# A list scheduler charges VectorE more, and the sums of a weight matrix are formed early in the kernel

## The chip, the cores and the metric

The kernel runs on one core of a Trainium2 chip. The metric is the device time of one execution in microseconds (us), the median of several runs. A core has five engines with a queue each: PE (TensorE, matrix products), DVE (VectorE), ACT (ScalarE), POOL (GpSimd) and SP (SyncE, which here only issues DMAs). Each engine works through its own list of instructions in order; semaphores make one wait for another.

## The reference, cut to what matters

One decoder layer over 1024 tokens of width 1024, in float32. Two causal token mixers read one projection of the normalised input: mixer A attends to the 256 best keys of each query, which an indexer chooses; mixer B is attention with a forgetting term. Both are gated, merged, and put through `w_out`.

```python
h = rmsnorm(x, g_pre[i])
proj = h @ w_in[i]
(qa, ka, va, gate_a, qi, ki, wi, qb, kb, vb, fb, gate_b) = jnp.split(proj, offs, axis=-1)
...
att_a = dsa_branch(qa, ka, va, qi, ki, wi).reshape(B, S, WIDTH_A)   # indexer scores, top-k, softmax attention
y_a = (att_a * jax.nn.silu(gate_a)) @ w_branch_a[i]
...
att_b = fox_branch(qb, kb, vb, log_f).reshape(B, S, WIDTH_B)
y_b = (att_b * jax.nn.silu(gate_b)) @ w_branch_b[i]
m_a, m_b = jnp.split(jax.nn.sigmoid(h @ w_merge[i]), 2, axis=-1)
out = (m_a * y_a + m_b * y_b) @ w_out[i]
x = x + rmsnorm(out, g_post[i])
e = p[i] @ w_ple[i]
gate = jax.nn.sigmoid(x @ w_ple_gate[i])
x = x + rmsnorm(gate * e, g_ple[i])
```

## The kernel before, in words

Every float32 product is made of three products of rounded parts (high by high, high by low, low by high; the helper `mm3`). So each operand is split first: one engine casts it to the high part, another subtracts that from the source to get the low part (`split_w`, `split_p`). Matrix products are up to 512 columns wide and write 128x512 results into one of eight PSUM banks.

The order of the work is not written by hand. The kernel records its operations (`Program.rec`), and `Program.schedule` then places them one by one on the five engines: a list scheduler, which keeps for each engine the time at which it comes free, and takes the operation that can start first (by priority where several can). How long an operation holds its engine it takes from `_cost`, in ns. For VectorE that is about 69 + 1.04 per column (85 + 1.04 per column for `tensor_tensor_reduce`), with 60 more for a per-partition scalar. To this come fixed latencies from engine to engine (`LAT`). Operations that two engines can do (`any`, `either`, `cast`, `split_w`) go to the one that the scheduler expects to finish first. The scheduler also gives every tile its place in three arenas, so all tiles have the names arena_r (rounded float32 in SBUF), arena_f (float32 in SBUF) and arena_p (PSUM) in the profile, and all instructions that it places have one line, L541.

The stages, in the order of time: the input is normalised, transposed and projected; the indexer's scores are made, with mixer B's value projection (`v_b`, PSUM tiles pv_0 to pv_7) between them; mixer A's query projection (`q_a`, tiles pa_0 to pa_7); then four pairs of heads of mixer B (`pair_b`), during which the top-k search (`top_k`) runs on ACT and DVE in 32 rounds: ACT counts five of the six score blocks against a threshold (`count`), DVE the sixth, and five operations of 6 columns on DVE choose the next threshold. Then come mixer A (`mixer_a`), the branch products, the product with `w_out` and the end. Two projections are filler for PE during the mixers, since nothing waits for them: mixer A's gate (`gates_a`) and the 16 merge gates (`merge_gates`).

The product with `w_out` is made of seven block products (Strassen's scheme in a variant of Winograd) and needs sums of blocks of `w_out`. `weight_sums` forms them: for each of four k, two DMAs bring 2 x 512 KB into a tile of 128x4x512, four subtractions of 128x512 work in it, and a DMA of 1 MB stores it to the DRAM tensor tw_d, which is read back near the end. Before, the subtractions are fixed to POOL (`G.tensor_sub`), and the loads may not start before merge gates 8 to 11 have been recorded as begun (`gate_at[8:12]`), in the late part of mixer A.

Of the kernel before, what the change touches and what calls it, by code (L numbers as in the profile page):

```python
# [150 lines left out]

def _cost(eng, method, a, k):

    if method == "dma_start":
        return 1000.0 if eng == "G" else 475.0
    out = k.get("out", a[0] if a else None)
# [8 lines left out]
    if eng == "A":  # L165
        c = n * 0.833 + 55
# [436 lines left out]
def hybrid_block_kernel(ctx: ExitStack, tc: tile.TileContext, x, p, w_in, b_forget, w_branch_a,  # L603
# [6 lines left out]
    pg = Program(tc, QUOTA)  # L610
    V, A, G, T, SY = pg.V, pg.A, pg.G, pg.T, pg.S
# [400 lines left out]
    def either(method, *a):  # L1012
        pg.any(("G", method, a, {}), ("V", method, a, {}))
# [157 lines left out]
    def q_a():  # L1171
        wqa = load_wn(C_QA, "wqa")
        for b in range(NB):
            psq = pg.psum([P, 512], "d", f"pa_{b}")
            nat_proj(psq, lambda k: wqa[k], b)
            for g in range(2):
                SY.dma_start(qsa_d[b][g], f(q_stack(psq[:, g * 256:g * 256 + 256], b, f"qa{b}{g}", 0.125)))

    def v_b():
        wvb = load_wn(C_VB, "wvb")  # L1180
        for b in range(NB):
            ps = pg.psum([P, 512], "d", f"pv_{b}")
            nat_proj(ps, lambda k: wvb[k], b)
            vt = pg.tile([P, 8, P], F32R, "vbt", f"vb{b}")
            split_p(ps.rearrange("p (h d) -> p h d", d=HD), vt[:, :, 0:HD], vt[:, :, HD:P])
            SY.dma_start(vb_d[:, b], f(vt))
# [73 lines left out]

    pg.at("vb", None)
    v_b()
    pg.at("qa", None)
    q_a()
    pg.at("ga", None)
    gates_a()
    pg.at("mg", None)
    merge_gates()
    pg.at("tw", None)
    tw_d = [pg.dram(dr, [P, 4, 4, 512], "tw_d0")]  # L1270

    def weight_sums(w, dst, after):
        for k in range(4):
            b4 = pg.tile([P, 4, 512], F32, "tw", f"tw{k}")
            for g in range(2):
                SY.dma_start(b4[:, 2 * g:2 * g + 2].rearrange("p a b -> p (a b)"), w[(4 * g + k) * P:(4 * g + k + 1) * P, :])
                pg.ops[-1].deps.add(after[k])
            G.tensor_sub(b4[:, 0], b4[:, 1], b4[:, 0])
            G.tensor_sub(b4[:, 1], b4[:, 3], b4[:, 1])
            G.tensor_sub(b4[:, 3], b4[:, 3], b4[:, 0])  # L1280
            G.tensor_sub(b4[:, 2], b4[:, 2], b4[:, 3])
            SY.dma_start(dst[:, k], b4)

    weight_sums(w_out[0], tw_d[0], gate_at[8:12])
    for pr in range(4):
        pg.at("pair", 1 + pr)
        pair_b(pr)
# [303 lines left out]
```

## Time and profile before

| | before |
|---|---|
| median of 3 runs | 1084.13 us (1083.5 to 1084.75) |
| profiled execution | 1086.23 us |
| its span, first to last instruction | 1084.3 us |
| PE busy | 1058.4 us (98%) |
| DVE busy | 822.1 us (76%) |
| ACT busy | 634.2 us (58%) |
| POOL busy | 122.6 us (11%) |
| mean granted clock of PE | 0.991 |

The busy time of an engine is the time in which one of its instructions ran. PE is busy in nearly all slices; its clock is granted at one of two levels, 1.00 (2.4 GHz) or 0.50 (1.2 GHz). The 1.9 us between the span and the profiled execution's time lie outside the instructions.

### The profile page before, as it was taken

How to read it: one execution, taken by the hardware profiler on the slowest of the kernel's cores; microseconds unless marked ns; L12 is line 12 of the kernel's file. 1: busy time of each engine (PE TensorE's matmuls, PEld its weight loads, DVE VectorE, ACT ScalarE, POOL GpSimd, SP SyncE). 2: the span in 40 equal slices, each digit the busy share in tenths (PEclk: the TensorE clock that was granted, in tenths of full speed). 3: DMA queues.
4: the chain of work that ended last, by engine and by line, in shares of the span. 5: the costliest groups of instructions: out<-in, count | busy, mean ns of one | idle time of the engine just before them, and what ended most of it. 6: DMA issues, size and time to landing. Idle time of an engine off the chain costs nothing. (4 is left out here: it accounts for less than half of the span.)

```text
span 1084.3 us, 16365 instructions
## 1 busy us (share of the span) xinstructions
PE 1058.4 (98%) x5266; PEld 873.1 (81%) x5266; DVE 822.1 (76%) x2136; ACT 634.2 (58%) x1454; POOL 122.6 (11%) x231
## 2 busy tenths in 40 slices
PE   8999999999999999999999999999999999999996
PEld 6887888887878778788787888778888888888885
DVE  7998777658868779889999976774358885598367
ACT  7576668888778788786348866544111243356222
POOL 2000000011201111211130110133010000000000
PEclk9999999999999999999999999999999999999998
DMA  7321143440551622815333431365597436536123
GB/s 250 89 60 49 75 159 108 153 101 20 135 119 59 146 69 69 194 40 186 107 108 116 119 88 59 113 227 204 169 308 237 141 119 211 181 110 197 38 97 117
DMA packets 119945, 139.51 MB, mean 129 GB/s; under 512 B 11819, under 2 KB 76715, under 8 KB 119349
## 3 DMA queue, kind: packets, MB, share of 16 engines
q1 hardware_dynamic: 108292, 120.13, 34.6%
q0 software_dynamic: 11568, 18.35, 7.4%
q8 instruction: 41, 0.67, 0.3%
q14 instruction: 44, 0.35, 0.1%
HBM read 96.94 MB, written 37.32 MB: 124 GB/s over the span
## 5 line engine op out<-in xcount | busy, mean ns | idle before, releaser
L541 PE MATMUL arena_p<-arena_r 128*128 128x512 f32 (+4 forms) x4360 | 1001.3, 384 | 14.3 <-DVE arena_r L541 6.8
L541 PEld LDWEIGHTS arena_p<-arena_r 128*128 128x128 f32 x4360 | 774.1, 189 | 170.0 <-ACT arena_f L541 9.8
L541 DVE TENSOR_TENSOR arena_r<-arena_p,arena_r 128x512 fp32r<-128x512 f32 (+2 forms) x232 | 142.4, 623 | 43.8 <-ACT arena_r L541 40.0
L541 ACT CAST arena_r<-arena_p 128x512 fp32r<-128x512 f32 (+3 forms) x217 | 107.5, 513 | 106.3 <-PE arena_p L541 97.8
L541 ACT ACTIVATE arena_f<-arena_p 128x512 f32<-128x512 f32 (+4 forms) x173 | 89.0, 525 | 129.9 <-PE arena_p L541 127.2
L541 ACT ACTIVATE arena_f<-arena_f,cnd 128x1024 bf16<-128x1024 f32 (+4 forms) x160 | 149.6, 935 | 23.6 <-DVE cnd L541 19.3
L541 DVE TENSOR_TENSOR arena_r<-arena_f,arena_r 128x512 fp32r<-128x512 f32 (+5 forms) x240 | 145.8, 622 | 12.8 <-PE arena_p L541 4.9
L541 ACT CAST arena_r<-arena_f 128x512 fp32r<-128x512 f32 (+3 forms) x144 | 80.4, 584 | 90.3 <-DVE arena_f L541 33.0
L541 ACT ACTIVATE arena_f<-arena_f,stats 128x512 f32<-128x512 f32 (+3 forms) x192 | 116.9, 611 | 27.4 <-DVE stats L541 26.6
L541 PE MATMUL arena_p<-ident,arena_f 128*128 128x128 f32 x720 | 108.7, 275 | 1.5 <-DVE arena_r L541 0.8
L541 PEld LDWEIGHTS arena_p<-ident,arena_f 128*128 128x128 f32 x720 | 87.2, 141 | 22.5 <-DVE arena_r L541 1.6
L541 POOL TENSOR_TENSOR arena_r<-arena_f,arena_r 128x512 fp32r<-128x512 f32 (+1 forms) x29 | 40.3, 1393 | 336.6 <-ACT arena_r L541 258.8
L541 DVE CAST arena_r<-arena_f 128x512 fp32r<-128x512 f32 (+4 forms) x125 | 47.7, 390 | 31.6 <-DMA arena_f<-in_w_out_dram 9.7
L541 DVE CUSTOM_DVE_ANT_0 arena_f<-arena_p,arena_f 128x512 f32<-128x512 f32 (+2 forms) x112 | 64.4, 578 | 7.6 <-PE arena_p L541 4.3
L541 DVE TENSOR_TENSOR arena_f<-arena_f 128x512 f32<-128x512 f32 (+3 forms) x132 | 64.9, 496 | 3.1 <-DMA arena_f<-rd_d 2.0
L541 ACT COPY arena_f<-arena_p 64x256 f32<-64x256 f32 (+5 forms) x94 | 42.5, 452 | 32.5 <-PE arena_p L541 27.3
L541 POOL TENSOR_SCALAR_AFFINE_SELECT arena_f<-arena_f 128x128 f32<-128x128 f32 x70 | 21.6, 309 | 314.2 <-DVE stats L541 112.7
L541 DVE CAST arena_r<-arena_p 128x512 fp32r<-128x512 f32 (+4 forms) x67 | 41.9, 626 | 19.8 <-PE arena_p L541 17.2
L541 DVE SCALAR_TENSOR_TENSOR arena_f<-arena_f,wi 128x384 f32<-128x384 f32 (+3 forms) x70 | 45.9, 657 | 12.7 <-ACT arena_f L541 12.1
L541 DVE SCALAR_TENSOR_TENSOR arena_f<-arena_f,arena_p 128x512 f32<-128x512 f32 x48 | 32.9, 685 | 24.9 <-PE arena_p L541 18.7
L541 DVE SCALAR_TENSOR_TENSOR arena_f<-arena_f 128x512 f32<-128x512 f32 (+8 forms) x48 | 29.3, 614 | 27.3 <-ACT arena_f L541 27.2
L541 ACT ACTIVATE arena_f<-arena_f 128x512 bf16<-128x512 f32 (+2 forms) x41 | 28.2, 687 | 27.1 <-DVE arena_f L541 24.5
(101 smaller groups left out, 514.8 us busy)
## 6 DMA issues: line engine op xcount, KB each, us to landing
arena_f<-in_w_in_dram SPq DMA_DIRECT2D x56, 256.0 KB, 3.7
arena_f<-in_w_merge_dram SPq DMA_DIRECT2D x32, 256.0 KB, 3.1
th_d<-arena_f SPq DMA_DIRECT2D x32, 256.0 KB, 2.0
arena_f<-th_d SPq DMA_DIRECT2D x32, 256.0 KB, 3.3
arena_f<-in_w_out_dram SPq DMA_DIRECT2D x14, 512.0 KB, 3.7
arena_f<-in_x_dram SPq DMA_DIRECT2D x18, 256.0 KB, 6.5
vb_d<-arena_r SPq DMA_DIRECT2D x8, 512.0 KB, 2.6
qsa_d<-arena_r SPq DMA_DIRECT2D x16, 256.0 KB, 2.4
```

Of the source, the lines that this page charges most:

```text
L541: getattr(eng[x], m)(*[real(q) for q in a], **{n: real(q) for n, q in k.items()})
```

## The change

`_cost` becomes `_hold`, and a new `_cost` wraps it: for VectorE an operation costs at least 100 ns, and one with an accumulator output (`accum_out`) costs 100 ns more. The other engines' costs stay as they are. The weight sums are recorded right behind `v_b`, their loads may start with the first four blocks of mixer B's value projection (`vb_at[:4]`), and each subtraction may go to POOL or VectorE (`either`). `gate_at` is still filled, and no longer read.

```diff
 def _cost(eng, method, a, k):

+    c = _hold(eng, method, a, k)
+    return max(c, 100.0) + (100.0 if "accum_out" in k else 0.0) if eng == "V" else c
+
+
+def _hold(eng, method, a, k):
     if method == "dma_start":
         return 1000.0 if eng == "G" else 475.0
...
+    vb_at = []
+
     def v_b():
         wvb = load_wn(C_VB, "wvb")
         for b in range(NB):
+            vb_at.append(len(pg.ops))
             ps = pg.psum([P, 512], "d", f"pv_{b}")
...
     pg.at("vb", None)
     v_b()
+    pg.at("tw", None)
+    tw_d = [pg.dram(dr, [P, 4, 4, 512], "tw_d0")]
+
+    def weight_sums(w, dst, after):
+        for k in range(4):
+            b4 = pg.tile([P, 4, 512], F32, "tw", f"tw{k}")
+            for g in range(2):
+                SY.dma_start(b4[:, 2 * g:2 * g + 2].rearrange("p a b -> p (a b)"), w[(4 * g + k) * P:(4 * g + k + 1) * P, :])
+                pg.ops[-1].deps.add(after[k])
+            either("tensor_sub", b4[:, 0], b4[:, 1], b4[:, 0])
+            either("tensor_sub", b4[:, 1], b4[:, 3], b4[:, 1])
+            either("tensor_sub", b4[:, 3], b4[:, 3], b4[:, 0])
+            either("tensor_sub", b4[:, 2], b4[:, 2], b4[:, 3])
+            SY.dma_start(dst[:, k], b4)
+
+    weight_sums(w_out[0], tw_d[0], vb_at[:4])
     pg.at("qa", None)
...
-            G.tensor_sub(b4[:, 0], b4[:, 1], b4[:, 0])
-            G.tensor_sub(b4[:, 1], b4[:, 3], b4[:, 1])
-            G.tensor_sub(b4[:, 3], b4[:, 3], b4[:, 0])
-            G.tensor_sub(b4[:, 2], b4[:, 2], b4[:, 3])
-            SY.dma_start(dst[:, k], b4)
-
-    weight_sums(w_out[0], tw_d[0], gate_at[8:12])
```

Since every later decision of the scheduler follows from the costs, nearly all lists change. The total of PE's instructions does not; 12 of POOL's 46 subtractions, additions and products go to DVE, and 20 casts go from DVE to ACT. Three places follow.

ACT's list, in the second pair of mixer B. `ACTIVATE arena_f,cnt` are counts of the search (128x1024 down to 128x512 are one round), `ACTIVATE arena_r<-arena_p 64x512 x2` empties a query projection out of its PSUM bank, `CAST arena_r<-arena_p` and `COPY` empty other banks. Before:

```order
L541 CAST arena_r<-arena_p 64x512
L541 CAST arena_r<-arena_f 128x512 x2
L541 ACTIVATE arena_f,cnt<-arena_f,cnd 128x1024
L541 ACTIVATE arena_f,cnt<-arena_f,cnd 128x896
L541 ACTIVATE arena_f,cnt<-arena_f,cnd 128x768
L541 ACTIVATE arena_r<-arena_p 64x512 x2
L541 ACTIVATE arena_f,cnt<-arena_f,cnd 128x640
L541 ACTIVATE arena_f,cnt<-arena_f,cnd 128x512
```

The same place now:

```order
L546 ACTIVATE arena_f,cnt<-arena_f,cnd 128x512
L546 ACTIVATE arena_f,cnt<-arena_f,cnd 128x1024
L546 ACTIVATE arena_r<-arena_p 64x512 x2
L546 ACTIVATE arena_f,cnt<-arena_f,cnd 128x896
L546 ACTIVATE arena_f,cnt<-arena_f,cnd 128x768
L546 ACTIVATE arena_f,cnt<-arena_f,cnd 128x640
L546 ACTIVATE arena_f,cnt<-arena_f,cnd 128x512
```

The emptying of the query projection stood behind three counts of its round, and stands behind one.

PE's list, in the third pair's key projection, while the second pair's last head is finished. `MATMUL arena_p<-ident,arena_f` are transposes of probabilities, of which `x4` opens the head's output, `128x512` are projections or the first products of probabilities and values. Before, the first of these products are the 4th and 5th of the row `x8`:

```order
L541 MATMUL arena_p<-ident,arena_f 128x128 x4
L541 MATMUL arena_p<-arena_r 128x128 x2
L541 MATMUL arena_p<-ident,arena_f 128x128 x3
L541 MATMUL arena_p<-arena_r 128x512 x6
L541 MATMUL arena_p<-ident,arena_f 128x128 x2
L541 MATMUL arena_p<-arena_r 128x512 x8
```

Now they are the 4th and 5th of the row `x14`:

```order
L546 MATMUL arena_p<-ident,arena_f 128x128 x4
L546 MATMUL arena_p<-arena_r 128x512 x3
L546 MATMUL arena_p<-arena_r 128x256 x2
L546 MATMUL arena_p<-ident,arena_f 128x128 x3
L546 MATMUL arena_p<-arena_r 128x128 x2
L546 MATMUL arena_p<-arena_r 128x512 x15
L546 MATMUL arena_p<-ident,arena_f 128x128 x2
L546 MATMUL arena_p<-arena_r 128x512 x14
```

Between the transposes and the product that needs them, split, stood 9 matmuls of 128x512 and stand 21.

SP's list, beside mixer B's value projection. `in_w_in_dram 128x512` are loads of the weights of mixer A's query projection, `128x4x128` of other projections, `vb_d` are stores of mixer B's values. Before, no load of `w_out` stands here:

```order
L541 DMA arena_f<-in_w_in_dram 128x4x128 x2
L541 DMA vb_d<-arena_r 128x1024
L541 DMA arena_f<-in_w_in_dram 128x512 x3
L541 DMA vb_d<-arena_r 128x1024
L541 DMA arena_f<-in_w_in_dram 128x512 x2
L541 DMA arena_f<-in_w_in_dram 128x4x128
```

Now the last two of four rounds of the weight sums read:

```order
L546 DMA arena_f<-in_w_out_dram 128x1024 x2
L546 DMA vb_d<-arena_r 128x1024 x2
L546 DMA arena_f<-in_w_in_dram 128x4x128 x2
L546 DMA tw_d_146<-arena_f 128x2048
L546 DMA arena_f<-in_w_out_dram 128x1024 x2
L546 DMA vb_d<-arena_r 128x1024
L546 DMA arena_f<-in_w_in_dram 128x512 x4
L546 DMA vb_d<-arena_r 128x1024 x2
L546 DMA tw_d_146<-arena_f 128x2048
L546 DMA arena_f<-in_w_in_dram 128x512
```

The last load of the query weights, the eighth, now stands behind the last store of the sums, and behind whatever that store waits for. All 16 subtractions of the sums are on DVE here, the last of them during the first matmuls of the query projection; in mixer A, POOL's rows `TENSOR_TENSOR arena_f<-arena_f 128x512 x4` and `x12` are gone.

## Rows read from the trace of the kernel before

**Rows 1.** Page: busy time of engines, and PE's clock in 40 slices.

```profile
PE 1058.4 (98%) x5266; PEld 873.1 (81%) x5266; DVE 822.1 (76%) x2136; ACT 634.2 (58%) x1454; POOL 122.6 (11%) x231
...
PEclk9999999999999999999999999999999999999998
```

**Rows 2.** Busy time by stage (count of instructions), PE's clock, DMA share, GB/s.

```profile
80.00:160.00 80.00, 80.00 (x376) 64.28 (x375) 60.98 (x131) 52.21 (x105) 1.57 (x4) 1.00 0.29 95
160.00:240.00 80.00, 80.00 (x391) 66.33 (x391) 52.77 (x204) 66.32 (x138) 4.83 (x8) 1.00 0.44 129
240.00:510.00 270.00, 261.20 (x1342) 216.26 (x1341) 221.09 (x634) 220.94 (x526) 44.16 (x96) 0.99 0.39 101
510.00:600.00 90.00, 88.06 (x430) 72.01 (x429) 84.06 (x201) 47.12 (x128) 17.79 (x16) 0.98 0.37 114
600.00:740.00 140.00, 137.06 (x699) 111.33 (x698) 105.13 (x275) 83.39 (x214) 28.67 (x30) 0.99 0.40 125
```

**Rows 3.** PE's timeline at five waits: start, length, what; idle before it.

```profile
248.62 0.65 PE L541 MATMUL arena_p<-arena_r 128*128 128x384 f32 x1 [2.39 <-DVE arena_f L541]
...
306.68 0.73 PE L541 MATMUL arena_p<-arena_r 128*128 128x512 f32 x1 [1.92 <-DVE arena_r L541]
...
365.67 0.50 PE L541 MATMUL arena_p<-arena_r 128*128 128x512 f32 x1 [0.97 <-DVE arena_r L541]
...
521.10 1.52 PE L541 MATMUL arena_p<-arena_r 128*128 128x128 f32 x5 [1.50 <-DVE stats L541]
...
725.13 1.19 PE L541 MATMUL arena_p<-arena_r 128*128 128x512 f32 x4 [1.96 <-DVE arena_r L541]
```

**Rows 4.** A stretch of 128x512 matmuls alone, and two stretches of lower clock.

```profile
760.00:800.00 40.00, 40.00 (x178) 33.14 (x177) 12.48 (x27) 5.73 (x11) 4.94 (x9) 1.00 0.71 217
...
306.70:310.10 3.40, 3.40 (x8) 2.72 (x9) 2.73 (x8) 3.31 (x7) 0.00 (x0) 0.50 0.40 96
...
726.60:730.00 3.40, 3.40 (x11) 2.72 (x10) 1.30 (x2) 0.60 (x1) 0.00 (x0) 0.50 0.39 154
```

**Rows 5.** Timeline ahead of the wait at 306.68, ACT and DVE.

```profile
301.83 1.04 ACT L541 ACTIVATE arena_f<-arena_f,cnd 128x896 bf16<-128x896 f32 x1
...
303.00 0.94 ACT L541 ACTIVATE arena_f<-arena_f,cnd 128x768 bf16<-128x768 f32 x1
...
303.93 1.18 ACT L541 ACTIVATE arena_r<-arena_p 64x512 fp32r<-64x512 f32 x2
...
305.15 1.39 DVE L541 SCALAR_TENSOR_TENSOR arena_r<-arena_p,arena_r 64x512 fp32r<-64x512 f32 x2 [3.24 <-ACT arena_r L541]
```

**Rows 6.** Timeline ahead of the wait at 725.13, DVE and POOL.

```profile
718.58 0.69 DVE L541 TENSOR_TENSOR arena_r<-arena_p,arena_r 128x512 fp32r<-128x512 f32 x1
719.18 0.68 DVE L541 TENSOR_TENSOR arena_f<-arena_f 128x512 f32<-128x512 f32 x1
...
720.00 5.61 POOL L541 TENSOR_TENSOR arena_f<-arena_f 128x512 f32<-128x512 f32 x4 [7.84 <-DMA th_d<-arena_f]
...
721.56 1.44 DVE L541 CAST arena_r<-arena_f 128x128 fp32r<-128x128 f32 x2
...
722.92 1.55 DVE L541 TENSOR_TENSOR arena_r<-arena_f,arena_r 128x128 fp32r<-128x128 f32 x2
```

**Rows 7.** Groups by shape: count, busy time, mean ns of one, idle before.

```profile
L541 DVE DVE_READ_ACCUMULATOR2_ANT stats<- 128x1 f32 x193 | 15.9, 82 | 0.0
...
L541 DVE CAST arena_r<-arena_f 128x128 fp32r<-128x128 f32 x25 | 6.3, 263 | 0.3 <-DMA va_d<-arena_r 0.3
```

**Rows 8.** DVE's timeline: a reduction, its accumulator's read, and the next reduction.

```profile
248.48 0.74 DVE L541 CUSTOM_DVE_ANT_0 arena_f<-arena_p,arena_f,stats 128x512 f32<-128x512 f32 x1
249.15 0.08 DVE L541 DVE_READ_ACCUMULATOR2_ANT stats<- 128x1 f32 x1
249.15 0.68 DVE L541 CUSTOM_DVE_ANT_0 arena_f<-arena_p,arena_f 128x512 f32<-128x512 f32 x1
```

**Rows 9.** Page, DMA issues: count, KB each, median us to landing.

```profile
arena_f<-in_w_in_dram SPq DMA_DIRECT2D x56, 256.0 KB, 3.7
```

More of the change, by code (lines that the diff above doesn't have):

```diff
@@ L1262, in hybrid_block_kernel @@
     v_b()
[L1263 to L1268, printed above, removed]
     pg.at("tw", None)
@@ L1277, in weight_sums @@
                 pg.ops[-1].deps.add(after[k])
-            G.tensor_sub(b4[:, 0], b4[:, 1], b4[:, 0])
-            G.tensor_sub(b4[:, 1], b4[:, 3], b4[:, 1])
-            G.tensor_sub(b4[:, 3], b4[:, 3], b4[:, 0])
-            G.tensor_sub(b4[:, 2], b4[:, 2], b4[:, 3])
+            either("tensor_sub", b4[:, 0], b4[:, 1], b4[:, 0])
+            either("tensor_sub", b4[:, 1], b4[:, 3], b4[:, 1])
+            either("tensor_sub", b4[:, 3], b4[:, 3], b4[:, 0])
+            either("tensor_sub", b4[:, 2], b4[:, 2], b4[:, 3])
             SY.dma_start(dst[:, k], b4)
-    weight_sums(w_out[0], tw_d[0], gate_at[8:12])
+    weight_sums(w_out[0], tw_d[0], vb_at[:4])
+    pg.at("qa", None)
+    q_a()
+    pg.at("ga", None)
+    gates_a()
+    pg.at("mg", None)
+    merge_gates()
     for pr in range(4):
```

## The prediction

> **What bounds the kernel now.** I read the page first: PE is busy for 98% of the span, at full clock in nearly every slice [rows 1]. So the change, which leaves PE's instructions as they are, can only win or lose what PE stands still or runs slowly; VectorE's and POOL's busy time count only where PE waits for them. Then I cut the busy time into stages [rows 2]: from 80 to 240 us PE has no idle time that the rows show, from 240 to 740 us, the two mixers, it lacks 8.80 + 1.94 + 2.94 = 13.7 us. The third view is PE's timeline at its long waits [rows 3]: five of them, 2.39, 1.92, 0.97, 1.50 and 1.96 us, make 8.7 of the 13.7 us, and all five are ended by VectorE. The other 5.0 us are many short waits. The fourth view is the clock. Behind the four waits of 1.50 us and more it is granted at 0.50, which is 1.2 GHz, for a stretch of 3.4 us each, of which two stand in [rows 4]. At full clock 178 matmuls of 128x512 take 40.00 us, 0.225 us each, so 3.4 us hold 15.1; behind the wait at 306.68 it held 8. The missing 7.1 cost 1.6 us; by the clock it is half of 3.4, 1.7 us, and I use 1.7. Four times that is 6.8 us. So 13.7 + 6.8 = 20.5 us is all that a better order can win between 240 and 740 us.
>
> **The new charges.** They put nothing on the chip; they move what the scheduler believes. A reduction of 512 columns out of PSUM starts at 248.48, and its accumulator's read and the next reduction both start at 249.15 [rows 8]: the read of 0.08 us lies beside the next instruction, and the engine is held for 0.67 us. The old charge (85 + 1.04 per column) is 0.617 us, the new one 0.717. An operation without an accumulator is charged 0.60 us as before, which is what [rows 6] show from start to start. The operations of 6 columns in the search go from 75 to 100 ns. So half of the added 100 ns is too much at least, and the scheduler now expects VectorE later than it will be. I take that as a margin: PE's list gets other work between a VectorE operation and the product that needs it. That is what the order shows in the third pair, 21 instead of 9 matmuls of 128x512 between the transposes and their product. 12 more at 0.225 us are 2.7 us, against a wait of 0.97 us. The margin is paid in filler: the gate projections are used up earlier, which costs nothing as long as some are left where mixer A ends.
>
> The Trainium skill, page "VectorE: DVE Perf Modes", section "Two Vector instructions with no wait between them", counts an operation with an accumulator output as two instructions, the operation and the read. If the second held the engine as the first does, the 193 reads in [rows 7] alone would hold it 15.9 us that the old charge leaves out; in rows 8 the next instruction doesn't wait for it. It is the third rival below.
>
> **The terms.** I go through the waits of [rows 3] and then through what is added.
>
> 1. Wait at 725.13, 1.96 us, and its clock. POOL runs four subtractions of the weight sums from 720.00 for 5.61 us; meanwhile two VectorE casts of 128x128 take 1.44 us and two subtractions of that size 1.55 us [rows 6], where a cast of this size takes 0.263 us over the run [rows 7]. These small operations are 2 us late, and the subtraction that PE's product needs stands behind them. The change takes the 16 subtractions off POOL and out of this stage, so nothing is left there to slow VectorE: 1.96 + 1.7 = 3.7 us won. What is late next there is the softmax chain on VectorE, which loses no time to POOL. The bounds are 0 and 3.7 us; I take 3.7.
>
> The Trainium skill, page "SBUF — State Buffer", section "Who interferes with whom", says that VectorE and GpSimd share one pair of ports as an exclusive lock held for a whole instruction. The trace agrees: each of the four small operations takes about half of a POOL subtraction's 1.40 us or more. By this rule a subtraction of two SBUF operands that is now on VectorE would wait only where POOL works; between 80 and 160 us POOL is busy 1.57 us [rows 2], so the sum stays. If the port were not the cause, this term would be 0 and the forecast 3.7 us later.
>
> 2. Wait at 306.68, 1.92 us, and its clock. PE needs a PSUM bank that ACT and VectorE empty together; VectorE's part waits 3.24 us for ACT, and ACT comes to it at 303.93, behind two counts that start at 301.83 and 303.00 [rows 5]. In the new list these two stand behind the emptying: it can start 303.93 - 301.83 = 2.1 us earlier, more than the wait. 1.92 + 1.7 = 3.6 us won; bounds 0 and 3.6. Late next is the search round, which nothing on PE waits for soon.
>
> 3. Wait at 248.62, 2.39 us. PE's list is nearly the same here, and one weight cast of 0.4 us has gone from VectorE to ACT. I take 0.4 us, and leave the clock as it is; bounds 0 and 2.39 + 1.7 = 4.1.
>
> 4. Wait at 365.67, 0.97 us: covered by the 12 matmuls above. 1.0 us; bounds 0 and 1.0.
>
> 5. Wait at 521.10, 1.50 us, first logits of mixer A behind VectorE's end of the search. VectorE is full here, 84.06 of 90 us [rows 2], before and after. The new list has more filler but the same load: I take half of 1.50 + 1.7, 1.6 us; bounds 0 and 3.2.
>
> 6. Added: the 16 subtractions, now all on VectorE, at 0.60 us from start to start [rows 6] are 9.6 us of its time, between about 95 and 160 us. VectorE's busy time from 80 to 160 us goes from 61.0 to 70.6 of 80 us [rows 2]. They stand between the indexer's scores, whose VectorE steps free buffers that ACT and PE need. The cover is the 19 us that VectorE idles there and the value projection, which PE can run ahead with. Nothing in the way is 0; all of it in the way is 9.6 us. PE shows no idle time there at 76% VectorE and loses 3% at 82% in the stage from 240 us, so at 88% I take 1.5 us, nearer to nothing.
>
> 7. Added: 4 MB of loads and 4 MB of stores on SP's queue there. The DMA share of 0.29 at 95 GB/s [rows 2] about doubles, with room left. Queued behind the last store are the eighth block of the query weights and the loads of later projections. The store waits for VectorE's last subtraction, and the load takes 3.7 us to land [rows 9]. PE's list runs the first products of several token blocks meanwhile, so I take 0 within the 1.5 us of term 6; its bound is one landing, 3.7 us. At the other end, the 4 loads and stores leave SP's queue in mixer A, which no row shows waiting on them: 0. Near the end tw_d is read long after its new time of storing: 0.
>
> 8. New waits of the new order. All later lists are rewritten, and some new pair of engines will meet badly. The nearest row is the rest of the idle time, 5.0 us; I take a quarter, 1.2 us, between 0 and 5.
>
> **The sum.** -3.7 - 3.6 - 0.4 - 1.0 - 1.6 + 1.5 + 1.2 = -7.6 us. The profiled execution took 1086.23 us, 1.9 us of it outside its span of 1084.3 us, and would take 1078.6 us with a span of 1076.7. The median of the runs shown is 2.1 us under it, 1084.13 us; from that the forecast is 1076.5 us. About 1071 to 1081 us is this case's own range.
>
> **The rivals.**
>
> Rival one, another order and no better one. The margin covers reads that hold nothing, so the new lists have as many waits as the old, at other places. For it: rows 8, and that four of the five waits come from chains over two engines which a charge on one engine does not describe. Against it: the two orders shown, in which the operation in the way has moved. Then only term 1 stays, less 1.5 us of term 6, and a new wait like that at 306.68 with its clock takes 3.6 back: about 1084.1 - 3.7 + 1.5 + 1.8 = 1083.7 us, with half of such a wait on average.
>
> Rival two, slower: the sums stand in PE's way. The place is 95 to 165 us; the mechanism is that each subtraction delays a score step, whose buffer PE needs, and that the last store holds the eighth weight block back. The price is all of 9.6 us, and two stops long enough for the lower clock, 3.4 us: 13.0 instead of 1.5 us. With the rest as forecast it is 1076.5 + 11.5 = 1088.0 us. It decides from the point where PE's idle time and clock loss from 80 to 240 us exceed 9.1 us, the gains of terms 1 to 5 less the rest. Against it: 19 us of idle VectorE time there.
>
> Rival three, VectorE was really undercharged, or the margin serves everywhere. Then the idle time of 13.7 us falls to a quarter, 3.4, the clock never falls, and term 8 is nothing: -10.3 - 6.8 + 1.5 = -15.6, 1068.5 us. For it: all five long waits are ended by VectorE. Against it: rows 8.
>
> **How the numbers follow.** 0.2% of the time, 2.2 us, is about what a measurement of this kernel can tell from no change: between 1081.9 and 1086.3 us is the same. The forecast gets 0.48, rival one 0.22, rival two 0.13, rival three 0.17. The forecast is faster but for 0.01; rival one is half the same (0.12), with 0.07 faster and 0.03 slower; rival two is slower with 0.10, the same with 0.02, faster with 0.01. Faster is 0.47 + 0.07 + 0.01 + 0.17 = 0.72, the same 0.01 + 0.12 + 0.02 = 0.15, slower 0.13. For 8 in 10 the range leaves out a third of rival three below 1067 us, half of rival two above 1088 us and the tails of the others.
>
> **What would show it.** Term 1: the stretch that holds the last blocks of mixer A has no lower clock, and the small casts there take 0.26 us. Terms 2 and 4: no wait of PE over 0.5 us at the second pair's gate projection and the third pair's key projection. Term 3: a wait near 250 us is still there. Term 6: VectorE near 70 us busy and PE's idle time from 80 to 160 us under 2 us. In sum, PE's idle time over the mixers near 7 us with one or two falls of the clock; four or more falls, or PE waiting over 5 us from 80 to 240 us, would make the prediction wrong.

## The result, and the profile after

The changed kernel takes 1077.63 us (median of 3 runs, 1076.64 to 1078.83) against 1084.13 us: a ratio of 0.994, interval 0.9915 to 0.9965. Beside further runs of the kernel before it read 0.9959, 0.9944 to 0.9973 (experiment 5). The forecast was 1076.5 us. The profiled execution took 1078.83 us with a span of 1077.1.

PE's instructions are the same 5266. The page's busy time and clock, to compare with [rows 1]:

```profile
PE 1051.3 (98%) x5266; PEld 871.0 (81%) x5266; DVE 824.9 (77%) x2128; ACT 638.4 (59%) x1474; POOL 114.8 (11%) x219
...
PEclk9999999999999999999999999999999999999998
```

PE's busy time falls by 7.1 us and the span by 7.2, so in sum PE idles as long as before: the same instructions take less time. The stages say more, to compare with [rows 2] (busy time and count of PE, PEld, DVE, ACT, POOL; clock; DMA share; GB/s):

```profile
80.00:160.00 80.00, 80.00 (x380) 64.41 (x380) 67.70 (x150) 52.75 (x107) 1.95 (x5) 1.00 0.50 167
160.00:240.00 80.00, 80.00 (x390) 65.73 (x389) 51.79 (x195) 65.41 (x137) 5.42 (x9) 1.00 0.55 163
240.00:510.00 270.00, 261.09 (x1352) 217.67 (x1351) 215.32 (x622) 224.88 (x536) 44.79 (x96) 0.99 0.39 99
510.00:600.00 90.00, 87.84 (x427) 71.80 (x426) 85.88 (x188) 44.77 (x119) 30.73 (x17) 1.00 0.40 121
600.00:740.00 140.00, 139.11 (x731) 116.16 (x730) 104.62 (x291) 90.22 (x239) 13.28 (x20) 1.00 0.32 95
```

From 80 to 160 us VectorE and the DMA do more and PE is still full. From 240 to 740 us PE lacks 8.91 + 2.16 + 0.89 = 12.0 us, where it lacked 13.7: only 1.7 us less. From 600 to 740 us it works through 731 instructions where it worked through 699, in the same time. In these two profiles the larger part is the clock, which fell behind four waits of the mixers before, and now behind one; the timed runs, read below, do not show that part.

The waits themselves, on PE's timeline (start, length, what; idle before it and what ended it), to compare with [rows 3]:

```profile
251.28 0.62 PE L546 MATMUL arena_p<-arena_r 128*128 128x384 f32 x2 [0.69 <-DVE stats L546]
...
311.40 0.50 PE L546 MATMUL arena_p<-arena_r 128*128 128x512 f32 x1 [2.14 <-DVE arena_r L546]
...
316.62 0.80 PE L546 MATMUL arena_p<-arena_r 128*128 128x512 f32 x1 [2.21 <-DVE arena_r L546]
```

The waits at 365.67 and 725.13 are gone, those at 248.62 and 521.10 are down to 0.69 and 0.56 us. The wait at 306.68 is not gone: it has become two. Behind the first the clock held, behind the second it fell, to compare with [rows 4]:

```profile
311.40:314.80 3.40, 3.01 (x12) 2.17 (x12) 2.13 (x5) 3.30 (x8) 0.00 (x0) 1.00 0.36 128
316.60:320.00 3.40, 3.38 (x8) 2.73 (x9) 3.29 (x10) 1.85 (x3) 0.00 (x0) 0.50 0.45 121
```

Why it stayed stands on VectorE's timeline, to compare with [rows 5]:

```profile
305.29 0.43 DVE L546 CAST arena_r<-arena_f 128x512 fp32r<-128x512 f32 x1 [3.40 <-DMA arena_f<-in_w_in_dram]
305.75 0.69 DVE L546 TENSOR_TENSOR arena_r<-arena_f,arena_r 128x512 fp32r<-128x512 f32 x1
306.36 0.16 DVE L546 TENSOR_TENSOR cnt<-cnt,thr_c 128x6 f32<-128x6 f32 x1
...
307.36 0.61 DVE L546 TENSOR_SCALAR_CACHE_REDUCE arena_f<-arena_f,cnd 128x384 bf16<-128x384 f32 x1
...
309.93 1.41 DVE L546 SCALAR_TENSOR_TENSOR arena_r<-arena_p,arena_r 64x512 fp32r<-64x512 f32 x2 [1.95 <-ACT arena_r L546]
```

And on ScalarE's:

```profile
302.49 0.72 ACT L546 ACTIVATE arena_f<-arena_f,cnd 128x512 bf16<-128x512 f32 x1
...
307.42 1.15 ACT L546 ACTIVATE arena_f<-arena_f,cnd 128x1024 bf16<-128x1024 f32 x1 [4.11 <-DVE cnd L546]
...
308.69 1.21 ACT L546 ACTIVATE arena_r<-arena_p 64x512 fp32r<-64x512 f32 x2
```

Read from the end: the emptying of the query projection (308.69, 309.93) stands behind the count at 307.42; that count waits 4.11 us for the search's threshold; the threshold (from 306.36) stands on VectorE behind the cast of the gate projection's weights, and the cast waits 3.40 us for its load. The load is issued at 296.06 and is used at 305.29, 9.2 us later, against 3.7 in [rows 9]. The DMA's busy share from 285 to 310 us, in 40 slices of tenths, gives the likely reason:

```profile
DMA  0105213000000009997998999999999999986200
```

From 294.4 to 307.5 us it is busy for 70% or more of every slice: the load goes together with the second pair's keys and values.

For every kernel below I cut the time at two instructions that all lists have: the first product of the value projection, and the first product of the output projection. "Start" is the time to the first, "middle" what lies between, from which half of every stretch of low clock between 240 and 740 us is then taken off. All from one profile each, in us; the ratio is of the timed runs.

| kernel | ratio | start | middle | lost by clock | middle without it |
|---|---|---|---|---|---|
| before | 1 | 91.9 | 812.7 | 6.8 | 805.9 |
| changed, two profiles | 0.994, 0.9959 | 95.0, 95.0 | 802.3, 801.6 | 1.7, 0 | 800.6, 801.6 |
| 1 new costs alone | 1.0058 | 95.1 | 814.1 | 5.1 | 809.0 |
| 2 sums moved alone | 0.9984 | 93.1 | 806.7 | 3.4 | 803.3 |
| 3 sums on VectorE in place | 0.9982 | 95.8 | 804.1 | 0 | 804.1 |
| 4 50 ns per read | 1.0021 | 93.0 | 808.5 | 3.4 | 805.1 |
| 6 cast behind | 0.9939 | 94.8 | 800.3 | 0 | 800.3 |
| 7 late filler | 1.0007 | 95.0 | 806.8 | 5.1 | 801.7 |
| 8 costs alone, cast behind | 1.0052 | 96.0 | 809.0 | 1.7 | 807.3 |
| 9 evictions first | 0.9930 | 95.2 | 798.5 | 0 | 798.5 |
| 10 least hold alone | 0.9984 | 93.8 | 803.0 | 0 | 803.0 |
| 11 200 ns per read | 0.9961 | 92.4 | 802.8 | 1.7 | 801.1 |
| 12 20 ns on the others | 1.0026 | 94.8 | 809.8 | 3.4 | 806.4 |

In these profiles the change wins 10.4 us in the middle, 5.1 of it clock. Of the other 5.3 us PE's rows show 1.7 as idle time; the rest lies in time that they count as busy. Its profile gives 3.1 us back at the start, where the lists are nearly alike: experiment 3, with the lists of before up to there, starts at 95.8. So the start scatters by 4 us from profile to profile, and the one of before was the earliest.

The clock needs more than one profile. The profiled execution of the kernel before has a mean granted clock of 0.991. Its 70 runs beside the experiments have 0.992 to 0.998, in the mean 0.9947; the ten runs of the changed kernel have 0.994 or 0.995, in the mean 0.9945. As an estimate, what is lacking to 1, times the span, is lost: 5.8 us before and 5.9 us after. So four falls in the mixers are that one profile's and not the kernel's, and the 4.6 us that experiment 5 gains are not clock. They are near the 4.3 to 5.3 us by which the table's last column falls. (Of the three runs of the kernel before behind the 6.5 us no clock is on record.)

### The profile page after: what moved, and what is told of

Same layout as the page of the kernel before. It is cut to its first block, busy times and chain, and to the rows that moved or that the text cites. A ratio compares the mean times of both kernels' runs of the same rounds, so it can differ in the third digit from the quotient of the medians.

```text
span 1077.1 us, 16338 instructions
## 1 busy us (share of the span) xinstructions
PE 1051.3 (98%) x5266; PEld 871.0 (81%) x5266; DVE 824.9 (77%) x2128; ACT 638.4 (59%) x1474; POOL 114.8 (11%) x219
## 4 chain that ended last, share of the span: by engine, by line
PE 77%; ACT 10%; DVE 7%; issue 2%; DMA 2%; POOL 1%; SPq 0%; ACTq 0%; DVEq 0%; POOLq 0%
PE arena_p L546 77%; ACT arena_f L546 7%; DVE arena_f L546 3%; DVE arena_r L546 3%; ACT arena_r L546 2%; DMA arena_f<-in_w_in_dram 1%; POOL arena_r L546 1%; DMA arena_f<-rd_d 1%; DVE cnd L546 0%; DMA rd_d<-arena_f 0%; SPq L546 0%; DVE add L546 0%; DVE cur L546 0%; ACT L546 0%; DVE stats L546 0%
## 5 line engine op out<-in xcount | busy, mean ns | idle before, releaser
L546 ACT CAST arena_r<-arena_p 128x512 fp32r<-128x512 f32 (+3 forms) x224 | 110.7, 516 | 99.9 <-PE arena_p L546 95.3
L546 DVE TENSOR_TENSOR arena_r<-arena_f,arena_r 128x512 fp32r<-128x512 f32 (+5 forms) x236 | 141.7, 617 | 6.3 <-ACT arena_r L546 3.3
L546 ACT CAST arena_r<-arena_f 128x512 fp32r<-128x512 f32 (+3 forms) x154 | 83.8, 571 | 90.2 <-DVE arena_f L546 35.6
L546 POOL TENSOR_TENSOR arena_r<-arena_f,arena_r 128x512 fp32r<-128x512 f32 (+2 forms) x33 | 53.9, 1640 | 380.0 <-ACT arena_r L546 223.1
L546 DVE TENSOR_TENSOR arena_f<-arena_f 128x512 f32<-128x512 f32 (+3 forms) x148 | 75.6, 518 | 6.3 <-DMA arena_f<-rd_d 5.5
L546 DVE CAST arena_r<-arena_f 128x512 fp32r<-128x512 f32 (+4 forms) x115 | 44.0, 389 | 18.0 <-DMA arena_f<-tw_d 7.5
L546 DVE CAST arena_r<-arena_p 128x512 fp32r<-128x512 f32 (+4 forms) x60 | 37.3, 621 | 18.4 <-PE arena_p L546 17.2
```

The lines of the kernel that those rows point to most:

```text
L546: getattr(eng[x], m)(*[real(q) for q in a], **{n: real(q) for n, q in k.items()})
```

## The experiments

Each ran beside the kernel before on the same chip, four kernels to a chip. Before took 1084.05, 1082.65 and 1081.96 us (medians) beside experiments 1 to 4, 5 to 8 and 9 to 12.

### 1. The new costs alone

```diff
+    c = _hold(eng, method, a, k)
+    return max(c, 100.0) + (100.0 if "accum_out" in k else 0.0) if eng == "V" else c
```

> The new charges for VectorE alone; the weight sums stay on POOL in mixer A, as before. Theory M (margin: PE gets other work between a VectorE step and the product that needs it): the waits of mixer B shrink, idle time plus half the time at the lower clock between 240 and 510 us falls from 12.2 to about 8 us, the waits by POOL's subtractions stay: about 1080 us. Theory P (all of the gain is the sums leaving POOL): 1084 us. Theory R (any new order gives new waits at other places, of about the same sum): anywhere from 1079 to 1089 us, and its gain and that of the sums alone do not add up to the change's 6.5 us.

1090.23 us, 1.0058 (1.004 to 1.0077): slower, and above all three ranges. PE's long waits, on its timeline:

```profile
310.65 0.70 PE L546 MATMUL arena_p<-arena_r 128*128 128x512 f32 x2 [4.31 <-DVE arena_r L546]
...
372.03 0.33 PE L546 MATMUL arena_p<-arena_r 128*128 128x128 f32 x1 [2.14 <-DVE arena_r L546]
...
477.00 0.44 PE L546 MATMUL arena_p<-ident,arena_f 128*128 128x128 f32 x2 [2.75 <-ACT arena_f L546]
...
488.51 0.55 PE L546 MATMUL arena_p<-ident,arena_f 128*128 128x128 f32 x3 [2.17 <-ACT arena_f L546]
```

The last two are of the fourth pair: transposes of probabilities wait for ScalarE's exponentials. In PE's list, the logits ahead of the first of them (`128x384`, `128x256` and the `128x512` of the next head) stand bare:

```
L546 MATMUL arena_p<-arena_r 128x512 x90
L546 MATMUL arena_p<-arena_r 128x384 x8
L546 MATMUL arena_p<-arena_r 128x256 x2
L546 MATMUL arena_p<-arena_r 128x512 x6
L546 MATMUL arena_p<-arena_r 128x384 x2
L546 MATMUL arena_p<-ident,arena_f 128x128 x16
```

In the changed kernel's list threes of the gate projection stand between them:

```
L546 MATMUL arena_p<-arena_r 128x384 x2
L546 MATMUL arena_p<-arena_r 128x512 x3
L546 MATMUL arena_p<-arena_r 128x384 x2
L546 MATMUL arena_p<-arena_r 128x512 x3
L546 MATMUL arena_p<-arena_r 128x384 x2
L546 MATMUL arena_p<-arena_r 128x512 x3
L546 MATMUL arena_p<-arena_r 128x384 x2
L546 MATMUL arena_p<-arena_r 128x512 x3
L546 MATMUL arena_p<-arena_r 128x256 x2
L546 MATMUL arena_p<-arena_r 128x512 x9
L546 MATMUL arena_p<-arena_r 128x384 x2
L546 MATMUL arena_p<-arena_r 128x512 x3
L546 MATMUL arena_p<-ident,arena_f 128x128 x8
```

Gate products are still left in experiment 1; they stand behind this stage. So the new costs by themselves are no margin that helps.

### 2. The sums moved alone

```diff
-    return max(c, 100.0) + (100.0 if "accum_out" in k else 0.0) if eng == "V" else c
+    return c
```

> The weight sums early and free to go to POOL or VectorE, with the old charges. M: term 1 alone, -3.7 us, and the waits of mixer B as before: about 1081 us. P: 1077 to 1078 us. R: anywhere from 1077 to 1088 us.

1083.27 us, 0.9984 (0.9969 to 0.9999), in theory R's range alone. The waits at 251.02 (1.92 us) and 312.89 (2.22 us) each have a clock fall. The two halves of the change, +0.6% and -0.2%, do not add up to -0.4 to -0.6%.

### 3. The lists of before, with the sums' 16 subtractions given to VectorE where they stand

```diff
                 if x == op.eng:
                     for m, a, k in calls:
+                    if x == "G" and calls[0][0] == "tensor_sub" and calls[0][1][0].t.name.startswith("tw"):
+                        x = "V"
```

> The lists of before, row by row, with the 16 subtractions of the weight sums issued on VectorE in place of POOL, at the same point in mixer A. Nothing else moves. M and P: the small casts near 721 us take 0.26 us again, PE's wait of 1.96 us and the lower clock behind it go: 3.7 us less, 1080.5 us. If POOL's subtractions are not the cause, or VectorE's 9.6 us more of work take their place: 1084 us or more, and a wait of PE in the same place.

1082.0 us, 0.9982 (0.9968 to 0.9996), between the two times that were expected. The stage of the wait at 725.13, in the kernel before:

```profile
700.00:740.00 40.00, 38.04 (x188) 30.84 (x187) 26.13 (x53) 18.11 (x42) 17.29 (x14) 0.96 0.67 223
```

and here:

```profile
700.00:740.00 40.00, 39.27 (x202) 31.65 (x201) 30.75 (x64) 18.52 (x41) 1.84 (x2) 1.00 0.70 229
```

POOL's 17.29 us are gone, VectorE has more to do, and PE waits less: its longest wait there is now 0.58 us. The four small operations of [rows 6], 1.44 and 1.55 us there, take 0.36 and 0.48:

```profile
720.06 0.36 DVE L543 CAST arena_r<-arena_f 128x128 fp32r<-128x128 f32 x2
720.33 0.48 DVE L543 TENSOR_TENSOR arena_r<-arena_f,arena_r 128x128 fp32r<-128x128 f32 x2
```

VectorE's casts of 128x128 take 219 ns in the mean over this run, 222 in the changed kernel, 263 in [rows 7]. So POOL's subtractions held these operations up. The Trainium skill, page "SBUF — State Buffer", section "Who interferes with whom", says that VectorE and GpSimd contend only for a pair of ports that they share, and that it is an exclusive lock. This run agrees, without showing that the ports are the place.

The same run says how far one profile goes. Nothing ahead of mixer A's late part is changed in it, and the waits of [rows 3] there come back as

```profile
252.55 0.62 PE L543 MATMUL arena_p<-arena_r 128*128 128x384 f32 x2 [2.39 <-DVE arena_f L543]
...
308.17 0.70 PE L543 MATMUL arena_p<-arena_r 128*128 128x512 f32 x2 [0.69 <-DVE arena_r L543]
...
520.93 0.95 PE L543 MATMUL arena_p<-arena_r 128*128 128x128 f32 x4 [1.50 <-DVE stats L543]
```

The second was 1.92 us. The clock fell behind all three in the profile of the kernel before, and behind none of them here.

### 4. 50 ns on a read, and no least hold

```diff
-    return max(c, 100.0) + (100.0 if "accum_out" in k else 0.0) if eng == "V" else c
+    return c + (50.0 if "accum_out" in k else 0.0) if eng == "V" else c
```

> The changed kernel with 50 ns instead of 100 ns more for an accumulator, which is what the trace shows for a reduction with a scalar, and without the least charge of 100 ns. M: half the margin, half the gain of mixer B: about 1079 us. R: anywhere from 1074 to 1086 us.

1086.26 us, 1.0021 (1.0007 to 1.0035), just above theory R's range and 7 us above theory M's time: half the charge is no half gain. The fourth pair's transposes wait again, and here too its logits stand bare:

```profile
477.25 0.98 PE L546 MATMUL arena_p<-ident,arena_f 128*128 128x128 f32 x7 [0.98 <-ACT arena_f L546]
...
488.89 0.33 PE L546 MATMUL arena_p<-ident,arena_f 128*128 128x128 f32 x1 [2.77 <-ACT arena_f L546]
```

### 5. The changed kernel again

The code is that of the change, with nothing edited.

> The changed kernel once more, for a narrower interval and to see which of its waits come back. Theory F (two places decide what a list is worth: the filler between a head's last logits and its transposes in the fourth pair, and a weight cast that stands ahead of evictions near 306 us): 0.994 of before, 0.992 to 0.996, the two waits near 311 and 317 us come back with 2.1 and 2.2 us, no wait over 0.5 us at the transposes of heads 6 and 7. Rival L (each list scatters its waits, and single profiles scatter too): the ratio anywhere from 0.992 to 0.998, waits of 311 and 317 us between 0.5 and 2.5 us.

1078.07 us, 0.9959 (0.9944 to 0.9973). The waits come back with 1.12 and 2.21 us near 310 and 315; this time the clock did not fall behind either. The ratio fits both theories, the 1.12 us only rival L.

### 6. One weight cast behind the threshold

The finished list is emitted in a new order: the two instructions get a later place, and everything else keeps its own, behind what it depends on and behind the last user of its buffer.

```diff
+    jv = next(i for i, op in enumerate(order) if any(t.name == "qb1_0" for t in op.tiles) and op.eng == "A")
+    for i, op in enumerate(order):
+        if any(t.name == "wgb1_0" for t in op.tiles) and op.eng == "V":
+            at[op] = jv - 0.5 + i * 1e-5
```

> The changed kernel with two instructions of VectorE moved in the finished list: cast and subtraction of the second pair's first gate weights go behind the five threshold operations and the first count that now follow them; every other list is unchanged. Theory F: ScalarE's 1024-column count starts near 304.4 instead of 307.4, the query projection's evictions end near 308 instead of 311.3, so the waits of 2.14 and 2.21 us shrink to under 1.3 and under 0.7 us, the clock fall at 316.6 goes (1.7 us): 3 to 5 us less than the changed kernel, about 1073.5, ratio to before 0.988 to 0.992. Rival L: the waits shrink there and come back behind (the search's counts and the next head's evictions now late), at most 1 us less than the changed kernel: 0.993 to 0.996.

1076.14 us, 0.9939 (0.9924 to 0.9953). PE's first wait is gone and the second is shorter:

```profile
307.80 4.01 PE L592 MATMUL arena_p<-arena_r 128*128 128x512 f32 x17
313.43 0.73 PE L592 MATMUL arena_p<-arena_r 128*128 128x512 f32 x2 [1.62 <-DVE arena_r L592]
```

On ScalarE the count starts at 304.23, as expected, and the second half of the query projection is emptied at 310.76, behind four counts:

```profile
304.23 1.15 ACT L592 ACTIVATE arena_f<-arena_f,cnd 128x1024 bf16<-128x1024 f32 x1 [1.10 <-DVE cnd L592]
...
305.50 1.21 ACT L592 ACTIVATE arena_r<-arena_p 64x512 fp32r<-64x512 f32 x2
...
310.76 1.20 ACT L592 ACTIVATE arena_r<-arena_p 64x512 fp32r<-64x512 f32 x2
```

So the cause named above is the cause of the first wait: two instructions later in one list take 3.33 us of waits down to 1.62 (from experiment 5). The time is 1.9 us less by the medians. That is between the two theories' numbers (3 to 5, at most 1); the ratio lies in rival L's range, and the ratios' intervals of experiments 5 and 6 overlap a little.

### 7. The fourth pair's filler moved behind the transposes

```diff
+    first = next(i for i, op in enumerate(pe) if of(op, "B6_6s0"))
+    last = next(i for i, op in enumerate(pe) if of(op, "Bv6_1t0"))
+    late = [op for op in pe if of(op, "pga3_1")]
+    spots = [op for op in pe[last + 1:] if not of(op, "pga3_1")]
+    for op, spot in zip(late, spots):
+        at[op] = at[spot] + 0.5
```

> The changed kernel with 24 matmuls of the fourth gate projection moved in TensorE's finished list: eight groups of three, six of which stood between head 6's second logits and its first transposes in the fourth pair, now stand one by one behind the first transposes of that half. All else is as in the changed kernel, so nothing but this cover is taken away (the work from head 6's first logits to its transposes falls from 10.2 to 6.1 us, in the kernel with the new costs alone it is 4.7). Theory F: a wait of 1.0 to 2.8 us appears at head 6's first transposes (0.98 and 2.75 us where the lists had no filler), with or without a clock fall (1.7 us): 1 to 4 us more than the changed kernel, ratio 0.995 to 0.998. Rival L: the logits and so the exponentials come earlier by as much, no wait over 0.6 us, within 0.7 us of the changed kernel.

1083.38 us, 1.0007 (0.9994 to 1.0021): 5.3 us more than experiment 5, the whole gain. The fourth pair in it:

```profile
470.00:475.00 5.00, 3.89 (x15) 2.30 (x14) 4.37 (x15) 4.35 (x10) 0.29 (x1) 1.00 0.00 0
475.00:482.00 7.00, 6.38 (x20) 5.00 (x20) 6.11 (x23) 6.69 (x22) 1.17 (x5) 0.51 0.25 76
```

and in the changed kernel (experiment 5):

```profile
470.00:475.00 5.00, 4.21 (x19) 3.14 (x18) 4.76 (x15) 4.52 (x10) 0.32 (x2) 1.00 0.00 0
475.00:482.00 7.00, 7.00 (x41) 6.13 (x40) 5.84 (x22) 7.00 (x21) 1.43 (x5) 1.00 0.25 76
```

Without the filler PE has three waits in a row for VectorE's reductions, which free the logits' banks. The first stands in the changed kernel too (0.79 us, at 473.62):

```profile
472.57 1.23 PE L597 MATMUL arena_p<-arena_r 128*128 128x512 f32 x4 [0.79 <-DVE arena_f L597]
474.12 1.32 PE L597 MATMUL arena_p<-arena_r 128*128 128x384 f32 x4 [0.32 <-DVE stats L597]
475.86 1.43 PE L597 MATMUL arena_p<-arena_r 128*128 128x384 f32 x4 [0.43 <-DVE stats L597]
```

Then the clock is at 1.2 GHz for 6.8 us from 475.1, and the expected wait at the transposes does not appear; it may be that at half speed the logits and transposes no longer catch up with the exponentials, which no run here tests. In this profile all of the loss is clock: in the table the middle is 806.8 us, and without its lost clock 801.7, that of experiment 5. 1.7 of its 5.1 us are a fall at 311.3, ahead of the moved instructions, where the changed kernel has a fall in one profile of two.

The timed runs say otherwise. This profile is the one of twelve runs with the lowest granted clock, 0.989. Eight of the twelve have 0.994 to 0.996, no less than the changed kernel's seven runs in experiment 5 (0.994 and 0.995), and take 1080.2 to 1085.06 us against 1076.27 to 1079.78. So of the 5.3 us, more than theory F's 1 to 4, some 4 come without any loss of clock; where PE loses them, no kept trace shows.

### 8. The new costs alone, with the weight cast behind the evictions

```diff
+    act = next(i for i, op in enumerate(order) if op.eng == "A" and of(op, "qb1_1"))
+    stt = next(i for i, op in enumerate(order) if op.eng == "V" and of(op, "qb1_1"))
+    for op in order:
+        if of(op, "wgb1_0") and op.eng in "AV":
+            at[op] = (act if op.eng == "A" else stt) + 0.5
```

> The kernel with the new costs alone, in whose list ScalarE's cast of the second pair's first gate weights and VectorE's subtraction behind it go behind the evictions of the query projection that now follow them. Theory F: the wait of 4.31 us at 310.65 shrinks to 2 to 2.7 us, and that much is gained, 1.5 to 4 us with the clock: ratio 1.002 to 1.0045 instead of 1.0058; the rest of its loss is the missing filler of the fourth pair (2.75 and 2.17 us stay at the transposes of heads 6 and 7). Rival L: no gain over 1 us, 1.005 to 1.007.

1088.38 us, 1.0052 (1.0033 to 1.0071). The wait of 4.31 us is gone altogether, more than expected; the waits of 2.75 and 2.17 us in the fourth pair stay. The ratio hardly moves (1.0058 before), though the profile's middle is 5.1 us shorter. 3.4 of these 5.1 us are clock. Undecided: the two ratios' intervals allow a gain of some 3 us as well as none.

### 9. Three evictions ahead of the search

```diff
+    for name, counts in (("pqb1_1", 2), ("pgb2_1", 1), ("pgb3_1", 1)):
...
+        for i in ja:
+            at[order[i]] = act[-1] + 0.5 + i * 1e-5
+        for i in range(step, stt[0]):
+            if order[i].eng == "V":
+                at[order[i]] = stt[-1] + 0.5 + i * 1e-5
```

> The changed kernel with, beside the moved weight cast of the run before, three evictions moved in ScalarE's and VectorE's finished lists ahead of one or two of the search's counts and of the threshold operations behind these: of the second half of the second pair's query projection, and of the second half of the gate projection in the third and the fourth pair. TensorE's list and all costs stay. Theory F (TensorE's remaining waits in mixer B come from evictions that stand behind the search): the waits of 1.65 us near 313, 1.14 near 396 and 0.8 near 469 us shrink under 0.4 each, 2.5 to 3.5 us less than with the cast alone, ratio to before 0.989 to 0.992, time near 1073. Rival L: the search then ends later, first waits move into mixer A or to the reductions of the logits, no more than 1 us less: 0.993 to 0.995.

1075.2 us, 0.993 (0.9915 to 0.9945), the lowest of all. It is rival L's ratio, and experiment 6 with the cast alone lies within its interval (0.9939): a gain by the three evictions is not shown. The second pair has no wait left in 15 us:

```profile
304.76 15.54 PE L604 MATMUL arena_p<-arena_r 128*128 128x512 f32 x66
```

In the third and the fourth pair the wait has moved two matmuls on, to the next reduction of VectorE, and is no shorter (1.16 and 0.79 us in experiment 6):

```profile
395.52 0.85 PE L604 MATMUL arena_p<-arena_r 128*128 128x384 f32 x3 [1.16 <-DVE stats L604]
...
469.33 0.85 PE L604 MATMUL arena_p<-arena_r 128*128 128x384 f32 x3 [0.94 <-DVE stats L604]
```

So one wait of three was only an eviction behind the search; at the other two VectorE's reductions are late as well.

### 10 to 12. Other charges, with the sums beside the value projection

```diff
-    return max(c, 100.0) + (100.0 if "accum_out" in k else 0.0) if eng == "V" else c
+    return max(c, 100.0) if eng == "V" else c                                            # 10
+    return max(c, 100.0) + (200.0 if "accum_out" in k else 0.0) if eng == "V" else c     # 11
+    return c + (0.0 if "accum_out" in k else 20.0) if eng == "V" else c                  # 12
```

> The changed kernel without the charge on the reads: weight sums beside the value projection, 100 ns as the least hold, no 100 ns on an accumulator. Its list keeps filler in the fourth pair (work between the last logits and the transposes of heads 6 and 7 3.4 and 3.6 us, in the changed kernel 3.1 and 4.4, with 50 ns 1.7 and 1.0), and the second pair's weight cast stands ahead of the search's counts. Theory F: about as good as the changed kernel, ratio 0.992 to 0.998, no wait over 0.8 us at those transposes. The margin theory as it was predicted (the charge on the reads is what gives TensorE its filler): like the kernel with the sums alone, 0.998 to 1.000. Rival L: no relation, anything from 0.992 to 1.006.

> The changed kernel with 200 ns instead of 100 ns on each read of an accumulator. Filler in the fourth pair: 3.4 us of work for head 6, 1.7 for head 7. Theory F: no wait at head 6's transposes, 0.5 to 2.5 us at head 7's, ratio 0.995 to 1.000. The margin theory as predicted (more margin costs only filler): 0.992 to 0.996. Rival L: anything from 0.992 to 1.006.

> The changed kernel with another charge that has nothing to do with reads or small operations: 20 ns on every VectorE operation without an accumulator, nothing on those with one, no least hold; the weight sums stay beside the value projection. Its list keeps filler in the fourth pair (3.4 and 2.7 us), but ScalarE's weight cast stands ahead of its counts and evictions in the second pair. Theory F: 0.994 to 0.999, a wait of 1.5 to 4 us near 310 us, none over 0.8 us at the transposes of heads 6 and 7. The margin theory: the wrong operations are charged, no better than the sums alone, 0.998 to 1.003. Rival L: anything from 0.992 to 1.006.

Experiment 10: 1081.2 us, 0.9984 (0.9972 to 0.9995). Experiment 11: 1078.54 us, 0.9961 (0.9947 to 0.9975). Experiment 12: 1085.37 us, 1.0026 (1.0013 to 1.0038). Theory F's ranges fail in experiments 10 (by 0.0004) and 12. Filler in the fourth pair does not tell these lists apart: none has a wait over 0.5 us at the transposes there. Their waits lie elsewhere; in experiment 12:

```profile
315.37 0.50 PE L546 MATMUL arena_p<-arena_r 128*128 128x512 f32 x1 [2.15 <-DVE arena_r L546]
...
467.46 0.50 PE L546 MATMUL arena_p<-arena_r 128*128 128x512 f32 x1 [1.68 <-DVE arena_f L546]
...
523.22 0.47 PE L546 MATMUL arena_p<-arena_r 128*128 128x128 f32 x1 [2.71 <-DVE stats L546]
```

With the sums moved, the charge on a read gives 0.9984 at 0 (experiments 2 and 10), 1.0021 at 50, 0.994 to 0.9959 at 100 and 0.9961 at 200 ns (experiments 2 and 4 without the least hold). All three expectations of the margin theory in this group held, that of experiment 11 at its edge; against it stand experiment 1 and that 50 ns are worse than none. A charge of 100 ns or more, or two lists that happened to come out well: five points do not settle it.

## Why the prediction was right, point by point

The side was right, and the time within 1.1 us; the way there was not, so that the second is largely luck. About 4.2 of the forecast's 7.6 us were to come from the clock: 1.7 each in terms 1 and 2, half of that in term 5. The two profiles show such a gain; the timed runs, with 0.9947 and 0.9945 in the mean, show none. Without it the sum is 3.4 us, and 4.6 to 6.5 were won: a gain that did not come and waits that were priced too low cancel. The margin, the reason for the new order's gains, is not shown.

- **What bounds the kernel** was right. PE's time in the middle decides, and the clock of one profile blurs it: in the table's last column every kernel with a ratio under 1 has up to 804.1 us, every one above 1 has 805.1 or more, but for experiment 7, profiled in its run of the lowest clock. But it is less the idle time than the prediction thought: that fell by 1.7 us.
- **Term 1** (3.7 us) was right in its mechanism: experiment 3 takes away nothing but POOL's part and the wait goes. As a time it measured 0.4 to 3.5 us, 2.0 in the middle: the wait of 1.96 us, without the 1.7 for the clock.
- **Term 2** (3.6 us) is the step that failed. "In the new list these two stand behind the emptying: it can start 303.93 - 301.83 = 2.1 us earlier" looked at ScalarE's list alone. The count that still stood ahead of the emptying hangs on VectorE's list, and there the cast of late weights had moved ahead of the threshold. The wait went from 1.92 to 2.14 + 2.21 us, and experiment 6 shows the cause of the first of them. The 1.92 us were partly that profile's: with the same lists experiment 3 has 0.69.
- **Terms 3 and 5** were too small. The waits fell by 1.70 and 0.94 us, and both lost their clock fall. The falls vary from run to run: in experiment 3, with the old lists, the 2.39 and 1.50 us came back without one.
- **Term 4** was right: the wait is gone. That the 12 matmuls are the reason was not tested.
- **Terms 6 and 7** were 0 instead of 1.5 us. VectorE is busy for 67.70 of 80 us (70.6 forecast), the DMA share rises from 0.29 to 0.50, and PE shows no idle time. The 19 us of idle VectorE time were cover enough.
- **Term 8** (1.2 us) was too small: waits of 1.14, 0.80 and 0.79 us near 400, 444 and 474 are new, and idle time over the mixers is 12.0 us, not 7. (The terms themselves add up to 13.7 - 6.0 + 1.2 = 8.9 us.) What made up for it in the profile was the clock, one fall, as forecast, against four that were the other profile's own.
- **The margin.** "Costs nothing as long as some are left where mixer A ends" is wrong. What counts is where filler stands: in experiment 7 24 matmuls of one gate projection, 18 of them (4.1 us of work) from ahead of the transposes, moved back by some places cost 4 to 5.3 us, though no filler was used up. The new costs alone lose 6 us.
- **The rivals.** Rival two fell with term 6. Rival three fell: idle time did not come near 3.4 us, and 200 ns were no better than 100. The Trainium skill, page "VectorE: DVE Perf Modes", section "Two Vector instructions with no wait between them", counts an operation with an accumulator output as two instructions; no run here shows a read that holds the engine as the operation does. Rival one is nearest to what experiments 1, 4 and 12 did: other lists, other waits.

What stays open is where most of the gain comes from. Experiment 3 explains about 2.0 of the 4.6 to 6.5 us, by POOL's subtractions. Why the charge and the moved sums are worth more together than apart, nothing here shows.

## What to carry to other kernels

Where a planner sets the order, a change of its costs is one draw of a list: plan on a scatter of some 15 us here (0.993 to 1.006 over eleven variants, five of them edits of a finished list), run several, and keep the best rather than the best argued. Follow a removed wait through every engine's list to a load or to PE itself before it is counted as won; the instruction behind which it waits next may be on another engine. Ask where filler stands, not only how much is left: 24 matmuls moved by some places cost 4 us or more here. A few instructions moved by hand in the finished list came out lower here (0.9939 and 0.993) than any further charge (0.9961 at best), though the intervals touch. And falls of the clock in one profile are no property of a kernel: compare the granted clock of all runs before a gain or a loss is put down to it.

## What was not expected of the hardware

- The clock fell behind three waits of 0.79, 0.32 and 0.43 us in a row (experiment 7), for 6.8 us, and it held behind one of 2.21 us (experiment 5) and one of 2.39 us (experiment 3). The same list lost it behind the wait near 316 us in one profile and not in the next, and the list of before lost it behind three waits of which two came back in experiment 3, as long and without a fall.
- The first product of the value projection starts between 91.9 and 96.0 us over fourteen profiles, with the same or nearly the same lists. Twelve show a stretch of 1.2 GHz from 11 to 13 us on, of 3.4 us in some and 6.8 in others; the two without one, of the kernel before and of experiment 11, are the two earliest.
- A load of 256 KB took 9.2 us from issue to use where the DMA was busy for 70% or more of every slice (profile after, from 294.4 to 307.5 us), against a median of 3.7 to landing.
